# Scaling of token tiles moved from VectorE to POOL in the first stage of a hybrid decoder step

## The chip, the cores and the metric

The kernel runs on one core of one Trainium2 chip. The metric is the time of one execution in device microseconds. Of the kernel before there are three timed runs, and one more execution that the hardware profiler recorded.

## The reference

One step of a one-layer decoder with two groups of heads side by side: stick-breaking attention (8 heads of 128) and gated linear attention (4 heads). 16 meta tokens, 1024 prompt tokens and 32 sample tokens (8 sequences of 4) go through the same layer; the sample tokens also attend to 1024 cached keys each. All numbers are float32. The part that matters here is the start, the norm of the input and the shared input projection:

```python
def rms_norm(x, g):
    xf = x.astype(jnp.float32)
    var = jnp.mean(xf * xf, axis=-1, keepdims=True)
    return (xf * lax.rsqrt(var + EPS) * g.astype(jnp.float32)).astype(x.dtype)
...
        h = rms_norm(x, norm_pre_g[l])
...
    u = h @ w_in
```

Here x has 1072 rows of 2048 numbers, and w_in has 2048 x 7184. The outputs are the new token rows, the new keys and values and the new states.

## The kernel before, in words

A float32 product is made of three faster ones: each operand is split into an upper half (its value rounded to the fp32r format) and a lower half (what the rounding left), and TensorE adds up upper x upper, upper x lower and lower x upper.

**First stage (lines 189 to 277).** The tokens lie in nine tiles, 0 to 8, of 128 rows (tile 0 has the 16 meta tokens ahead of 112 prompt rows; tile 8 has the last 16 prompt rows and the 32 sample rows, folded so that it needs one buffer of 1024 columns instead of two). `load_x(i)` (line 197) issues a tile's transfers. For tile 8 POOL first clears rows that no transfer fills (a memset, line 201), and the transfers of the sample rows on the SP queue (line 210) wait for it. `norm_x(i)` (line 215) makes the tile's norm and scales it:

- ScalarE squares each piece and sums it up (line 225), and VectorE adds up the pieces (line 227). For tile 8 VectorE also adds the two folded halves (lines 231 to 233).
- `rstd_` (line 156) makes one over the root: a multiply-add on VectorE (line 162), a logarithm and an exponential on ScalarE (lines 163, 164), and four tiny VectorE operations that refine it (lines 165 to 168).
- line 236 multiplies the tile by this number, row by row, in place: two instructions of 128 x 1024 (one of 112 x 1024 for tile 8).

Three groups of tiles, c = 0, 1, 2 (tiles 0-2, 3-5, 6-8), follow one another. In each, for 16 blocks of 128 columns, TensorE transposes the block of three tiles into a PSUM buffer `tx` (line 260; five such buffers), ScalarE copies it to SBUF times the weight `gpre`, which is the upper half in `hT` (line 261), and VectorE makes the lower half from the same PSUM buffer (line 262). A `tx` buffer is free for a later block when line 262 has read it. The products with the first 128 columns of w_in (`acc_v`, lines 272 to 274) are mixed in among the transposes. `NORMS` (line 238) says behind which block which tile's `norm_x` is written: tile 3 behind block 1 of group 0, tiles 4 and 5 behind its blocks 4 and 10, tiles 6, 7 and 8 behind blocks 2, 5 and 8 of group 1. Tiles 0 to 2 are scaled ahead of everything.

**What sets the order.** Each engine works through its own queue in order. The code's order is a start only: a scheduler places the instructions of all engines by priorities and by the times it expects, so an edit of one line moves others. Weight loads are marked urgent. The constants' transfers (lines 140 to 144) are on SP behind tile loads and weight loads; among them is nbal (line 141, 128 x 4 numbers), which VectorE negates (line 142) at a place in its queue amid the lower halves.

Behind this stage come the other column blocks of w_in (lines 279 to 295), with the attention work woven in, and then the output projection. The DVE of the profile is VectorE, ACT is ScalarE, PE is TensorE, SP is the queue that issues most transfers.

Of the kernel before, what the change touches and what calls it, by code (L numbers as in the profile page):

```python
# [16 lines left out]
ALU = mybir.AluOpType  # L17
# [65 lines left out]
def hybrid_step(ctx: ExitStack, tc: tile.TileContext, x_prompt, x_sample, cache_k, cache_v, state_gla,  # L83
# [5 lines left out]
    vec, act, pool = nc.vector, nc.scalar, nc.gpsimd  # L89
# [66 lines left out]
    def rstd_(pl, ssq, n, rows, w, nm):  # L156

        v = pl.tile([P, w], F32, tag="rs_v", name=f"v_{nm}")
        r = pl.tile([P, w], F32, tag="rs_r", name=f"r_{nm}")
        t = pl.tile([P, w], F32, tag="rs_t", name=f"t_{nm}")  # L160
        v, r, t = v[:rows], r[:rows], t[:rows]
        vec.tensor_scalar(v, ssq, 1.0 / n, EPS, ALU.mult, ALU.add)
        act.activation(r, v, AF.Ln)
        act.activation(r, r, AF.Exp, scale=-0.5)
        vec.tensor_tensor(t, r, r, ALU.mult)
        vec.tensor_tensor(t, t, v, ALU.mult)
        vec.tensor_scalar(t, t, -0.5, 1.5, ALU.mult, ALU.add)
        vec.tensor_tensor(r, r, t, ALU.mult)
        return r
# [20 lines left out]
    with tc.tile_pool(name="xp", bufs=2) as xp, tc.tile_pool(name="xps", bufs=5, space=PSUM) as xps:  # L190
# [24 lines left out]
        def norm_x(i):  # L215
            xt = xts[i]
            rows = P if i < 8 else 112
            w = H if i < 5 else 512 if i < 8 else 256
            q = len(xt) * H // w
            ssq = xp.tile([P, 4], F32, tag="ssq", name=f"ssq{i}")  # L220
            for e in range(q):
                j0 = 0 if i < 5 else (448 if i < 8 else 768) + 1088 * (e % 2)
                jk = hT[15][:rows, j0:j0 + w]
                xe = xt[e * w // H][:rows, e * w % H:e * w % H + w]
                act.activation(jk, xe, AF.Square, accum_out=ssq[:rows, e:e + 1])
            sq = xp.tile([P, 1], F32, tag="sq", name=f"sq{i}")
            vec.tensor_reduce(sq[:rows], ssq[:rows, :q], mybir.AxisListType.X, ALU.add)
            if i == 8:
                other = xp.tile([P, 1], F32, tag="so", bufs=1, name="so")
                pool.memset(other[:], 0.0)  # L230
                vec.tensor_copy(other[0:48], sq[64:112])
                vec.tensor_copy(other[64:112], sq[0:48])
                vec.tensor_tensor(sq[:rows], sq[:rows], other[:rows], ALU.add)
            r = rstd_(xp, sq[:rows], D, rows, 1, f"x{i}")
            for t in xt:
                vec.tensor_scalar(t[:rows], t[:rows], r, None, ALU.mult)

        NORMS = {(0, 1): 3, (0, 4): 4, (0, 10): 5, (1, 2): 6, (1, 5): 7, (1, 8): 8}
        for i in range(5):
# [6 lines left out]
        for i in range(3):  # L246
            norm_x(i)
        for c, (lo, hi) in enumerate(CHUNKS):
            n = hi - lo
            for k in range(NK):  # L250
                ps = xps.tile([P, 384], F32, tag="tx", name=f"tx{c}_{k}")
                ks = slice(k % 8 * P, (k % 8 + 1) * P)
                for j in range(3):
                    xt = xts[3 * c + j]
                    if len(xt) == 2:
                        src, ii = xt[k // 8][:, ks], ident[:]
                    else:
                        rs = slice(64 * (k // 8), 64 * (k // 8) + 48)
                        src, ii = xt[0][rs, ks], ident[rs, rs]
                    nc.tensor.transpose(ps[:, j * P:min((j + 1) * P, n)], src, ii)  # L260
                act.activation(hh[k][:, lo:hi], ps[:, :n], AF.Copy, scale=gpre[:, k:k + 1])
                vec.scalar_tensor_tensor(hl[k][:, lo:hi], ps[:, :n], gpre[:, k:k + 1], hh[k][:, lo:hi].bitcast(F32),
                                         ALU.mult, ALU.subtract)
                if c == 0 and k == 7:
                    load_x(5)
                if (c, k) in NORMS:
                    norm_x(NORMS[c, k])
            lo, hi = SCHUNKS[c]
            o_ = first[c][:, :hi - lo]
            for k in range(NK):  # L270
                wh, wl = (t[:, k % 2, :] for t in wchunks[k // 2])
                mm(o_, wh, hh[k][:, lo:hi], start=(k == 0), stop=False)
                mm(o_, wh, hl[k][:, lo:hi], start=False, stop=False)
                mm(o_, wl, hh[k][:, lo:hi], start=False, stop=(k == NK - 1))
            if c == 0:
                for i in (6, 7, 8):
                    load_x(i)
# [1264 lines left out]
```

## Time and profile before

| what | us |
|---|---|
| median of three runs | 2131.66 |
| lowest and highest of them | 2129.86, 2132.66 |
| the profiled execution's own time | 2132.25 |
| its span, first to last instruction | 2130.5 |
| TensorE busy in the span | 2066.0 (97%) |
| VectorE busy | 1573.2 (74%) |
| ScalarE busy | 994.4 (47%) |
| POOL busy | 81.9 (4%) |

The span is the time from the first to the last instruction; the execution's own time has 1.75 us around it. Shares of busy time are means over all stages. What the first stage does is read from the timeline of its first 74 us, where each row gives an instruction's start, its length, and in brackets how long its engine had stood idle ahead of it and which instruction or transfer ended that.

### The profile page before, as it was taken

How to read it: one execution, taken by the hardware profiler on the slowest of the kernel's cores; microseconds unless marked ns; L12 is line 12 of the kernel's file. 1: busy time of each engine (PE TensorE's matmuls, PEld its weight loads, DVE VectorE, ACT ScalarE, POOL GpSimd, SP SyncE). 2: the span in 40 equal slices, each digit the busy share in tenths (PEclk: the TensorE clock that was granted, in tenths of full speed). 3: DMA queues.
4: the chain of work that ended last, by engine and by line, in shares of the span. 5: the costliest groups of instructions: out<-in, count | busy, mean ns of one | idle time of the engine just before them, and what ended most of it. 6: DMA issues, size and time to landing. Idle time of an engine off the chain costs nothing.

```text
span 2130.5 us, 43361 instructions
## 1 busy us (share of the span) xinstructions
PE 2066.0 (97%) x12546; PEld 1868.5 (88%) x12546; DVE 1573.2 (74%) x6592; ACT 994.4 (47%) x2536; POOL 81.9 (4%) x298
## 2 busy tenths in 40 slices
PE   5999999999999999999999999999999999999997
PEld 5999999999999989999898998998888887777775
DVE  6368888889888889898897888977544446453575
ACT  7345556565555656424435345353434335342332
POOL 0000000100001010200000000000000000000000
PEclk9999999999999999999999999999999999999999
DMA  6234443444444354554443444336667666452484
GB/s 198 72 100 126 129 129 108 135 130 114 132 131 123 104 143 115 163 132 114 120 121 111 134 116 132 94 86 186 206 220 236 216 190 195 134 154 76 128 286 168
DMA packets 380442, 304.02 MB, mean 143 GB/s; under 512 B 50410, under 2 KB 320682, under 8 KB 380202
## 3 DMA queue, kind: packets, MB, share of 16 engines
q1 hardware_dynamic: 378010, 300.97, 48.6%
q8 instruction: 99, 1.62, 0.3%
q14 instruction: 141, 1.16, 0.2%
q10 hardware_dynamic: 2192, 0.27, 0.1%
HBM read 243.39 MB, written 57.72 MB: 141 GB/s over the span
## 4 chain that ended last, share of the span: by engine, by line
PE 81%; DVE 8%; DMA 7%; issue 2%; ACT 2%; SPq 1%; POOL 0%; DVEq 0%; ACTq 0%; POOLq 0%
PE acc_g L289 4%; PE b L1451 4%; PE acc_g L291 4%; PE acc_g L290 4%; PE b L1452 4%; PE b L1453 4%; PE acc_k L289 3%; PE acc_k L290 3%; PE acc_k L291 3%; PE acc_q L289 3%; PE acc_q L290 3%; PE acc_q L291 3%; PE acc_gv L289 3%; PE acc_gv L290 3%; PE acc_gv L291 3%; PE acc_v L289 3%
## 5 line engine op out<-in xcount | busy, mean ns | idle before, releaser
L384 DVE SCALAR_TENSOR_TENSOR jk<-kp,qb 128x128 f32<-128x128 f32 x2048 | 591.1, 289 | 39.0 <-DMA qb<-qsd 2.0
L289 PE MATMUL acc_g<-hT,wh_g 128*128 128x368 f32 (+2 forms) x768 | 252.9, 329 | 3.2 <-ACT gx L438 3.1
L291 PE MATMUL acc_g<-hT,wl_g 128*128 128x368 f32 (+2 forms) x768 | 247.3, 322 | 0.0
L290 PE MATMUL acc_g<-hT,wh_g 128*128 128x368 f32 (+2 forms) x768 | 247.2, 322 | 0.0
L1451 PE MATMUL b<-ring,f 128*128 128x512 f32 x416 | 166.6, 402 | 6.0 <-ACT gx L438 2.9
L289 PEld LDWEIGHTS acc_g<-hT,wh_g 128*128 128x128 f32 x768 | 144.3, 188 | 28.7 <-ACT wh_g L184 15.9
L1315 DVE TENSOR_TENSOR ring<-wr,ring 128x512 fp32r<-128x512 f32 x104 | 70.7, 690 | 133.0 <-ACT ring L1314 132.4
L384 DVE DVE_READ_ACCUMULATOR jk<-kp,qb 128x1 f32 x2048 | 166.5, 81 | 0.0
L1452 PE MATMUL b<-ring,f 128*128 128x512 f32 x416 | 163.1, 392 | 0.9 <-DVE ring L1315 0.9
L1453 PE MATMUL b<-ring,f 128*128 128x512 f32 x416 | 162.8, 391 | 0.0
L291 PEld LDWEIGHTS acc_g<-hT,wl_g 128*128 128x128 f32 x768 | 144.3, 188 | 1.6 <-issue 1.6
L290 PEld LDWEIGHTS acc_g<-hT,wh_g 128*128 128x128 f32 x768 | 144.4, 188 | 1.0 <-issue 0.3
L1314 ACT CAST ring<-wr 128x512 fp32r<-128x512 f32 x104 | 64.3, 621 | 163.9 <-DMA wr<-in_w_out_dram 79.4
L289 PE MATMUL acc_gv<-hT,wh_gv 128*128 128x384 f32 (+1 forms) x384 | 129.2, 336 | 0.0
L289 PE MATMUL acc_k<-hT,wh_k 128*128 128x378 f32 (+1 forms) x384 | 127.6, 332 | 0.0
L290 PE MATMUL acc_k<-hT,wh_k 128*128 128x378 f32 (+1 forms) x384 | 125.4, 326 | 0.0
L289 PE MATMUL acc_q<-hT,wh_q 128*128 128x368 f32 (+2 forms) x384 | 125.3, 326 | 0.0
L291 PE MATMUL acc_gv<-hT,wl_gv 128*128 128x384 f32 (+1 forms) x384 | 125.3, 326 | 0.0
L291 PE MATMUL acc_k<-hT,wl_k 128*128 128x378 f32 (+1 forms) x384 | 125.2, 326 | 0.0
L290 PE MATMUL acc_gv<-hT,wh_gv 128*128 128x384 f32 (+1 forms) x384 | 124.7, 325 | 0.0
L290 PE MATMUL acc_q<-hT,wh_q 128*128 128x368 f32 (+2 forms) x384 | 123.6, 322 | 0.0
L291 PE MATMUL acc_q<-hT,wl_q 128*128 128x368 f32 (+2 forms) x384 | 123.5, 322 | 0.0
(427 smaller groups left out, 5401.7 us busy)
## 6 DMA issues: line engine op xcount, KB each, us to landing
kp<-in_cache_k_dram SPq DMA_DIRECT2D x512, 64.0 KB
vr<-in_cache_v_dram SPq DMA_DIRECT2D x64, 512.0 KB
tf<-in_w_out_dram SPq DMA_DIRECT2D x64, 256.0 KB
qb<-qsd SPq DMA_DIRECT2D x64, 256.0 KB
td<-tf SPq DMA_DIRECT2D x64, 256.0 KB
wr_g<-in_w_in_dram SPq DMA_DIRECT2D x128, 128.0 KB
wr<-td SPq DMA_DIRECT2D x64, 256.0 KB
wr<-in_w_out_dram SPq DMA_DIRECT2D x48, 256.0 KB
```

Of the source, the lines that this page charges most:

```text
L289: mm(acc[c][:, :n], wh[:, k2, :], hh[k][:, lo:hi], start=(k == 0), stop=False)
L290: mm(acc[c][:, :n], wh[:, k2, :], hl[k][:, lo:hi], start=False, stop=False)
L291: W.mark = mm(acc[c][:, :n], wl[:, k2, :], hh[k][:, lo:hi], start=False, stop=(k == NK - 1)).ins
L384: ins = vec.scalar_tensor_tensor(jk[:], kp[:], 1.0, qbs[h, b][:, t, :], ALU.mult, ALU.mult, accum_out=zt[:, t, NPG - 1 - i:NPG - i])
L1314: act.copy(wh, r)
L1315: vec.tensor_tensor(wl, r, wh.bitcast(F32), ALU.subtract)
L1451: mm(bk[:], ah, wh, start=first and k == 0, stop=False, skip_group_check=True)
L1452: mm(bk[:], ah, wl, start=False, stop=False, skip_group_check=True)
L1453: mm(bk[:], al, wh, start=False, stop=last and k == 7, skip_group_check=True)
```

## The change

One line of `norm_x`: tiles 0 to 2 are still scaled by VectorE, tiles 3 to 8 by POOL.

```diff
@@ -233,7 +233,7 @@
             r = rstd_(xp, sq[:rows], D, rows, 1, f"x{i}")
             for t in xt:
-                vec.tensor_scalar(t[:rows], t[:rows], r, None, ALU.mult)
+                (vec if i < 3 else pool).tensor_scalar(t[:rows], t[:rows], r, None, ALU.mult)
```

With it the scheduler moves other instructions of this stage; behind the stage every engine's order is as it was, and SP's order is the same throughout.

POOL, from the end of the identity matrix on. The names `x_0_` and `x_1_` are the two halves of a tile's row: 233 and 234 are tile 3, 237 and 238 tile 4, 374 and 375 tile 5, and 501 is tile 8.

```order
 masks.py:199 AFFINE_SELECT ident<-ident 128x128
+L236 TENSOR_SCALAR x_0_233<-x_0_233,r_x_310 128x1024
+L236 TENSOR_SCALAR x_1_234<-x_1_234,r_x_310 128x1024
+L236 TENSOR_SCALAR x_0_237<-x_0_237,r_x_345 128x1024
+L236 TENSOR_SCALAR x_1_238<-x_1_238,r_x_345 128x1024
 L201 MEMSET x_0_501 32x1024
+L236 TENSOR_SCALAR x_0_374<-x_0_374,r_x_404 128x1024
+L236 TENSOR_SCALAR x_1_375<-x_1_375,r_x_404 128x1024
```

The memset for tile 8, which was POOL's first instruction behind the identity, now stands behind four scalings. Behind the rows shown come the two scalings of tile 6, the two of tile 7 and the one of tile 8.

VectorE, at the change from group 0 to group 1. `hT_162` is the last block of group 0, `hT_147`, `hT_148`, `hT_149` are the first three of group 1; `sq_530` and `v_x_532` belong to the norm of tile 6.

```order
 L262 SCALAR_TENSOR_TENSOR hT_162<-tx_15_439,gpre,hT_162 128x384
-L167 TENSOR_SCALAR t_x_405<-t_x_405 128x1
-L168 TENSOR_TENSOR r_x_404<-r_x_404,t_x_405 128x1
-L236 TENSOR_SCALAR x_0_374<-x_0_374,r_x_404 128x1024
-L236 TENSOR_SCALAR x_1_375<-x_1_375,r_x_404 128x1024
+L262 SCALAR_TENSOR_TENSOR hT_147<-tx_0_507,gpre,hT_147 128x384
+L142 TENSOR_SCALAR nbal<-nbal 128x4
+L262 SCALAR_TENSOR_TENSOR hT_148<-tx_1_513,gpre,hT_148 128x384
+L262 SCALAR_TENSOR_TENSOR hT_149<-tx_2_519,gpre,hT_149 128x384
 L227 TENSOR_REDUCE sq_530<-ssq_525 128x1
 L162 TENSOR_SCALAR v_x_532<-sq_530 128x1
-L142 TENSOR_SCALAR nbal<-nbal 128x4
```

Tile 5's scaling is gone from here (its norm's last steps stand earlier now). The operation on nbal moved behind the first lower half of group 1, and tile 6's sum and variance moved behind nbal and two more lower halves.

ScalarE, at the same place. The `L225` rows are the squares of tile 6, `r_x_533` its norm.

```order
 L225 ACTIVATE hT_162,ssq_525<-x_0_493 128x512 x2
-L225 ACTIVATE hT_162,ssq_525<-x_1_494 128x512 x2
+L225 ACTIVATE hT_162,ssq_525<-x_1_494 128x512
 L261 ACTIVATE hT_147<-tx_0_507,gpre 128x384
 L261 ACTIVATE hT_148<-tx_1_513,gpre 128x384
 L261 ACTIVATE hT_149<-tx_2_519,gpre 128x384
+L225 ACTIVATE hT_162,ssq_525<-x_1_494 128x512
+L261 ACTIVATE hT_150<-tx_3_544,gpre 128x384
+L261 ACTIVATE hT_151<-tx_4_550,gpre 128x384
 L163 ACTIVATE r_x_533<-v_x_532 128x1
-L261 ACTIVATE hT_150<-tx_3_544,gpre 128x384
+L261 ACTIVATE hT_152<-tx_5_556,gpre 128x384
```

The last of tile 6's four squares moved behind the first three copies of group 1, and the logarithm of its norm behind two more. On TensorE the transposes of tile 5's first two blocks moved ahead, among group 0's last products, and two of tiles 3 and 4 went behind them; on VectorE the operation of line 233 (tile 8's two halves) moved ahead of group 1's tenth lower half, and TensorE transposes tile 8's first block as its third transpose of group 2, where it stood behind seven others.

## The prediction

> **What bounds the kernel now.** I read the page's head, then TensorE's waits in the first 74 us (where every instruction of the change lies), the chain of waits, and the busy time stretch by stretch.
>
> ```profile
> span 2130.5 us, 43361 instructions
> PE 2066.0 (97%) x12546; PEld 1868.5 (88%) x12546; DVE 1573.2 (74%) x6592; ACT 994.4 (47%) x2536; POOL 81.9 (4%) x298
> ```
>
> TensorE is busy 97% of the span. So the change is worth what it takes from TensorE's idle time between 26 us (first edited scaling) and 58 us. These are TensorE's rows around its waits there, in the timeline (start, length, idle time before, releaser):
>
> ```profile
> 36.31 0.44 PE L272 MATMUL acc_v<-hT,wf 128*128 128x378 f32 x1 [1.75 <-ACT hT L261]
> 41.38 0.27 PE L260 MATMUL tx<-ident,x 128*128 128x128 f32 x1
> 44.84 0.55 PE L260 MATMUL tx<-ident,x 128*128 128x128 f32 x3 [1.30 <-DVE hT L262]
> 53.57 0.55 PE L260 MATMUL tx<-ident,x 128*128 128x128 f32 x3 [0.84 <-DVE hT L262]
> 57.99 2.13 PE L260 MATMUL tx<-ident,x 128*128 128x128 f32 x14
> ```
>
> Two waits, 1.30 and 0.84 us, end with VectorE: 2.14 us is what VectorE can give at most. The 1.75 us ends with ScalarE, and behind that stands a transfer of weights, which the change doesn't touch; the second row is a stretch of time (busy PE, PEld, DVE, ACT, POOL, then granted clock, DMA share, GB/s):
>
> ```profile
> 34.94 0.84 ACT L184 CAST wh_k<-wr_k 128x256 fp32r<-128x256 f32 x2 [1.37 <-DMA wr_k<-in_w_in_dram]
> 37.60:41.20 3.60, 3.60 (x16) 3.42 (x15) 3.42 (x10) 3.54 (x12) 0.00 (x0) 0.53 1.04 202
> ```
>
> After that pause TensorE had 0.53 of its clock for 3.6 us, which costs it 3.6 x 0.47 = 1.7 us. Both stay: in the new order one small ScalarE instruction (L163 for tile 5, 0.2 us) goes ahead of the copy that ends the pause, no more. Should the new order bring a second pause of that kind, 1.7 us is its price. The other stretches:
>
> ```profile
> 44.00:46.00 2.00, 1.16 (x9) 1.13 (x10) 1.90 (x6) 1.69 (x6) 0.00 (x0) 1.00 0.00 0
> 46.00:52.00 6.00, 6.00 (x44) 5.71 (x43) 5.83 (x18) 5.97 (x23) 0.00 (x0) 1.00 0.00 0
> 52.00:54.00 2.00, 1.16 (x9) 0.85 (x8) 1.92 (x7) 2.00 (x5) 0.00 (x0) 1.00 0.00 0
> 58.00:74.00 16.00, 16.00 (x98) 12.92 (x97) 8.91 (x19) 8.68 (x19) 1.00 (x8) 1.00 0.00 1
> ```
>
> From 44 to 54 us ScalarE is as full (9.66 of 10) as VectorE (9.65); from 58 us on TensorE has no gap. The chain there, in order of time:
>
> ```profile
> 37.69 6.39 DMA nbal<-in_b_alpha_dram
> 44.10 0.17 DVE nbal L142
> 44.27 1.57 DVE hT L262 x3
> 47.71 1.42 DVE x L236 x2
> 51.51 1.42 DVE x L236 x2
> 52.99 0.54 DVE hT L262
> ```
>
> VectorE stands still until the tiny transfer of nbal lands at 44.1, since L142 waits for it at the head of its queue; then two scaled pairs (2.84 us) lie on the chain.
>
> **The change: VectorE.** One line's instructions (min/median/max ns):
>
> ```profile
> L236 DVE TENSOR_SCALAR x<-x,r_x x17: 746/752/755, 12.2 to 57.8; 128x1024 f32<-128x1024 f32 x16, 112x1024 f32<-112x1024 f32 x1
> ```
>
> Eleven of the 17 leave VectorE: 11 x 0.75 = 8.3 us, 2.84 of it on the chain. No transfer, copy or matmul goes away.
>
> **POOL's price** for such a scaling is not in the trace. Its nearest rows (mean ns behind the bar), and the memset ahead of tile 8:
>
> ```profile
> L1096 POOL MEMSET vn<- 128x1024 f32 x1 | 0.9, 947 | 0.0
> L517 POOL TENSOR_SCALAR_AFFINE_SELECT X<-X 127x126 f32<-127x126 f32 x48 | 14.3, 298 | 66.9 <-DVE X L514 63.7
> L517 POOL TENSOR_SCALAR_AFFINE_SELECT X<-X 25x24 f32<-25x24 f32 x8 | 1.6, 204 | 183.4 <-DVE X L514 183.4
> L704 POOL TENSOR_SCALAR_AFFINE_SELECT lv<-lv 128x64 f32<-128x64 f32 x14 | 6.0, 452 | 0.1
> 33.48 1.31 POOL L201 MEMSET x<- 32x1024 f32 x1 [32.10 <-PE tx L260]
> ```
>
> Lower end: a write of the same width, which reads nothing, 0.95 us. Through the two L517 rows a pass that reads and writes costs 0.18 + 0.92 ns a column: 1.1 us for 1024, the value I take. Upper end: L704 takes 1.9 times that line (0.45 for 0.24), so 2.1 us. Call the price s.
>
> **Where a slow POOL shows first.** SP issues nbal behind tile 8's transfers, which wait for that memset, and POOL's memset now stands behind tile 4's two scalings.
>
> ```profile
> 26.51 1.42 DVE L236 TENSOR_SCALAR x<-x,r_x 128x1024 f32<-128x1024 f32 x2
> 32.28 0.16 DVE L168 TENSOR_TENSOR r_x<-r_x,t_x 128x1 f32<-128x1 f32 x1
> 39.61 0.16 DVE L168 TENSOR_TENSOR r_x<-r_x,t_x 128x1 f32<-128x1 f32 x1
> 34.81 0.89 SPq L210 DMA_DIRECT2D x<-in_x_sample_dram  x2
> 35.83 0.90 SPq L180 DMA_DIRECT2D wr_k<-in_w_in_dram  x2
> ```
>
> The first row is tile 3's pair, the L168 rows end tile 4's and tile 5's norms. Tile 4's is ready at 32.4, and some 0.4 earlier without tile 3's pair ahead: 32.0 (an estimate). SP issued nbal at 37.69 (chain, above). The memset ends at 32.0 + 2s + 0.95 instead of 34.8; SP needs 1.9 us from there until it is free for nbal (34.81 to 36.73), and stood idle for 0.96 more. With s = 1.1 it ends at 35.15: 0.36 late, nbal on time, cost nothing. With s = 2.1 nbal is 1.4 us late, and VectorE, ScalarE and TensorE with it. With s = 0.95 nothing is gained by it, since SP stood idle before nbal already. Queued behind nbal on SP are two tiny transfers and then cache pages, which wait for the end of this stage.
>
> **What goes, and what is late next.** VectorE now makes the first lower half (hT_147) ahead of its wait for nbal, so TensorE's next three transposes and two matmuls (44.84 to 45.57, 0.73 us) go into its 1.30 us wait. But the other wait hangs on ScalarE too:
>
> ```profile
> 42.47 1.52 ACT L261 ACTIVATE hT<-tx,gpre 128x384 fp32r<-128x384 f32 x3 [1.33 <-PE tx L260]
> 45.90 0.62 ACT L225 ACTIVATE hT<-x 128x512 fp32r<-128x512 f32 x1
> 48.36 1.03 ACT L261 ACTIVATE hT<-tx,gpre 128x384 fp32r<-128x384 f32 x2
> 51.68 3.05 ACT L261 ACTIVATE hT<-tx,gpre 128x384 fp32r<-128x384 f32 x6
> ```
>
> TensorE now transposes tile 5 where the lone transpose of 41.38 stood, so ScalarE's copies start at about 41.5, not 42.47. (Tile 5 must be scaled by then: its norm was there at 39.77, plus 1.1 is 40.9.) Three copies (1.52), the one square of tile 6 that is moved behind them (0.62) and two copies (1.0) bring it to 44.6. There L163 for tile 6 now waits for VectorE: nbal at 44.27, two halves (1.05), reduce and scale (0.3) give 45.6. Then L163 and L164, a copy (0.9 together) and tile 7's squares, which start at about 46.5 instead of 45.90. So everything behind is 0.6 us later on ScalarE, and its copy of 51.68 starts at 52.3. That copy (0.5) and its lower half (0.54) end at 53.4, where the chain has 53.53. The 0.84 us wait hardly shrinks; the 0.73 us is given back as another wait. Sum of the likeliest case: -0.1 to -0.3, I take **-0.2 us**.
>
> Tile 8 is the last that could be late: its scaling ended VectorE's part at 58.5 (row below); POOL has it at about 56.2 + 1.1, ahead of TensorE's need at 58. POOL's five scalings from tile 6's norm on (row at 47.53) end at 47.5 + 5s, so they are late only from s = 2.1.
>
> ```profile
> 47.53 0.15 DVE L168 TENSOR_TENSOR r_x<-r_x,t_x 128x1 f32<-128x1 f32 x1
> 57.77 0.76 DVE L236 TENSOR_SCALAR x<-x,r_x 112x1024 f32<-112x1024 f32 x1
> 313.08 0.69 POOL L517 TENSOR_SCALAR_AFFINE_SELECT X<-X 33x32 f32<-33x32 f32 x1 [13.35 <-DVE X L514]
> 313.08 0.41 DVE L185 TENSOR_TENSOR wl_v<-wr_v,wh_v 128x256 fp32r<-128x256 f32 x1
> ```
>
> **Contention.** The last two rows: a POOL select of 33x32 took 0.69 while VectorE ran a two-input operation of 0.41; the 25x24 ones above take 0.20. The two can hold each other up. VectorE's L233, two inputs, now stands ahead of the half of 52.99 while tile 7 is scaled: 0 to 1.1 us late, and I count 0. The Trainium skill (SBUF — State Buffer, Who interferes with whom) speaks against the change: a VectorE operation with two SBUF inputs and a POOL operation that reads SBUF exclude each other for a whole instruction. The trace agrees (0.69 for 0.20); by that rule the sum would be up to +0.9.
>
> So the bounds are -0.73 (none given back) and +1.4 + 1.1 = +2.5. The profiled execution took 2132.25 us, 1.75 over its span, 0.59 above the median of 2131.66; -0.2 makes it 2132.05, and the median **2131.5**.
>
> **Rivals.**
> 1. VectorE alone was the limit and both waits go: -2.1, 2129.5. For it: both end with L262. Against it: ScalarE's 9.66 of 10. Chance 0.10.
> 2. POOL is so slow that it becomes the bound: with s above 2.1 nbal is 2s - 2.8 late and tile 8 another 5s - 10.5. At s = 2.5 that is 2.2 + 2.0 = 4.2, which is 0.2%; at 3.0 it is 3.2 + 4.5 = 7.7: 2139.4. For it: a POOL pass with a scalar by partition is nowhere in the trace. Against it: 1.1 by the L517 rows. Chance of s above 2.5: 0.07; between 1.5 and 2.5 (2132 to 2136): 0.10.
> 3. POOL's first such instruction starts late by some t, as if code had to be fetched: tile 4 is then done at 26.5 + t + 4s, the memset 0.95 and nbal's issue another 1.9 later, so with s = 1.1 nbal is late by t - 3.9. Rows of a first use (POOL's first select, ScalarE's load of its table):
>
> ```profile
> 1.08 0.29 POOL masks.py:199 TENSOR_SCALAR_AFFINE_SELECT ident<-ident 128x128 f32<-128x128 f32 x1
> 1.73 1.28 ACT L97 ACT_TABLE_LOAD   x1 [1.73 <-PEq L1523]
> ```
>
> The first select took what later ones take, so t = 0; with ScalarE's load, t = 1.3, nothing is late either: 2131.5. From t = 8.2 on it passes 4.3 us: 2135.9. Chance that t is above 3.9: 0.03. The Trainium skill (GPSIMD Engine Reference, Instruction dispatch) gives about 6 us for the first call of a freshly loaded library; by that it would be 2.1 us, 2133.8, and no row here shows such a load.
>
> That nothing moves is excluded: POOL's order has all eleven scalings, and VectorE's has none of them left.
>
> **How the numbers follow.** My case has 0.68, the rivals 0.30, anything else 0.02. About 0.2% (4.3 us) is what a measurement of this kernel can tell from no change. Faster by that would need more than the 2.14 us: 0.03. Slower: rival 2 beyond 2.5 and a little else, 0.08. Same: 0.89. The range takes in rival 1 and, with the runs' own spread (2129.86 to 2132.66), the slower POOL: 2128.8 to 2135.
>
> **What would show it.** Right: eleven L236 rows on POOL near 1.1 us; nbal issued near 37.7; TensorE's 0.84 us wait replaced by one ended by ScalarE, and 58 to 74 us as full. Wrong: POOL rows above 2 us, nbal late, or TensorE at its 57.99 row over 1 us earlier.

## The result, and the profile after

| | before | after |
|---|---|---|
| median of 6 runs, us | 2132.02 | 2147.00 (2143.69 to 2152.38) |
| profiled execution, us | 2132.25 | 2146.43 |
| its span, us | 2130.5 | 2144.7 |
| mean granted TensorE clock | 0.994 | 0.989 |

After takes 1.0076 of before, with an interval of 1.0065 to 1.0087: 15 us slower, where 2131.5 was forecast and the range ended at 2135. The head of the page of after:

```profile
span 2144.7 us, 43378 instructions
PE 2077.1 (97%) x12546; PEld 1875.4 (87%) x12546; DVE 1568.1 (73%) x6581; ACT 994.7 (46%) x2536; POOL 112.3 (5%) x309
```

TensorE has the same 12546 matmuls and is busy 11.1 us longer (2066.0 before): most of the loss is not idle time but the same work done slower. The change's own line in after (min/median/max ns, first and last start):

```profile
L236 POOL TENSOR_SCALAR x<-x,r_x x11: 2842/2846/2964, 26.5 to 59.0; 128x1024 f32<-128x1024 f32 x10, 112x1024 f32<-112x1024 f32 x1
L236 DVE TENSOR_SCALAR x<-x,r_x x6: 745/750/753, 12.3 to 18.6; 128x1024 f32<-128x1024 f32 x6
```

A scaling costs 2.85 us on POOL and 0.75 us on VectorE. The forecast took 1.1 us, with 2.1 as its upper end. POOL's timeline in after (start, length, idle time before, releaser):

```profile
26.49 5.67 POOL L236 TENSOR_SCALAR x<-x,r_x 128x1024 f32<-128x1024 f32 x2 [25.12 <-DVE r_x L168]
32.37 5.79 POOL L236 TENSOR_SCALAR x<-x,r_x 128x1024 f32<-128x1024 f32 x2 [0.21 <-ACT hT L225]
38.21 0.94 POOL L201 MEMSET x<- 32x1024 f32 x1
39.25 5.67 POOL L236 TENSOR_SCALAR x<-x,r_x 128x1024 f32<-128x1024 f32 x2
47.72 14.13 POOL L236 TENSOR_SCALAR x<-x,r_x 128x1024 f32<-128x1024 f32 x5 [2.80 <-ACT hT L225]
```

The last row is tiles 6, 7 and 8 without a gap: five scalings end at 61.85. TensorE's timeline around them:

```profile
45.02 0.55 PE L260 MATMUL tx<-ident,x 128*128 128x128 f32 x3 [0.24 <-DVE hT L262]
53.31 0.55 PE L260 MATMUL tx<-ident,x 128*128 128x128 f32 x3 [0.35 <-DVE v_x L162]
57.61 0.27 PE L260 MATMUL tx<-ident,x 128*128 128x128 f32 x1
61.90 3.80 PE L260 MATMUL tx<-ident,x 48*128 48x48 f32 x13 [4.03 <-POOL x L236]
87.91 0.33 PE L289 MATMUL acc_k<-hT,wh_k 128*128 128x378 f32 x1
```

The two waits that ended with VectorE are down from 1.30 and 0.84 us to 0.24 and 0.35. TensorE reaches group 2 (the third group of token tiles, 6 to 8) at 57.61, the place that stands at 57.99 in before; after one more transpose it has nothing to do for 4.03 us until tile 8 is scaled. Behind that, the stretches of time (columns: busy PE, PEld, DVE, ACT, POOL, then granted clock, DMA share, GB/s):

```profile
58.00:74.00 16.00, 12.10 (x40) 7.70 (x41) 5.34 (x10) 5.31 (x11) 4.55 (x5) 0.63 0.00 1
61.90:86.00 24.10, 24.10 (x82) 17.45 (x83) 8.54 (x16) 9.16 (x18) 0.70 (x3) 0.50 0.00 1
86.00:88.00 2.00, 2.00 (x15) 2.00 (x15) 0.33 (x2) 0.03 (x1) 0.31 (x5) 0.99 0.00 0
```

For 24.1 us TensorE is busy without a gap, at half its clock; before, 58 to 74 us stood at 1.00. The ledger up to acc_k's first matmul (87.91; before 73.76):

- TensorE reaches group 2 at 57.61 instead of 57.99: -0.4.
- It goes on at 61.90, after one transpose and the wait of 4.03 us: +4.3.
- Group 2 takes 61.90 to 87.91 = 26.0 instead of 57.99 to 73.76 = 15.8: +10.2.

The sum is +14.1, and the span of the profiled execution is 14.2 longer: in the end nothing is given back later.

### The profile page after: what moved, and what is told of

Read it like the earlier page. It is cut to its first block, busy times and chain, and to the rows that moved or that the text cites. A ratio compares the mean times of both kernels' runs of the same rounds, so it can differ in the third digit from the quotient of the medians.

```text
span 2144.7 us, 43378 instructions
## 1 busy us (share of the span) xinstructions
PE 2077.1 (97%) x12546; PEld 1875.4 (87%) x12546; DVE 1568.1 (73%) x6581; ACT 994.7 (46%) x2536; POOL 112.3 (5%) x309
## 4 chain that ended last, share of the span: by engine, by line
PE 85%; DVE 6%; DMA 5%; ACT 2%; issue 1%; POOL 1%; SPq 0%; DVEq 0%; ACTq 0%; POOLq 0%
PE acc_g L289 5%; PE acc_g L291 5%; PE acc_g L290 5%; PE b L1451 4%; PE b L1452 4%; PE b L1453 4%; PE acc_k L289 3%; PE acc_k L290 3%; PE acc_k L291 3%; PE acc_q L289 3%; PE acc_q L290 3%; PE acc_q L291 3%; PE acc_v L289 3%; PE acc_gv L289 3%; PE acc_gv L290 3%; PE acc_gv L291 3%
## 5 line engine op out<-in xcount | busy, mean ns | idle before, releaser
L289 PEld LDWEIGHTS acc_g<-hT,wh_g 128*128 128x128 f32 x768 | 144.9, 189 | 28.8 <-ACT wh_g L184 14.2
```

The costliest lines, as they stand in the source:

```text
L289: mm(acc[c][:, :n], wh[:, k2, :], hh[k][:, lo:hi], start=(k == 0), stop=False)
```

## The experiments

The theory after the result: POOL is slow enough that tile 8 is late, that pauses TensorE, and the pause brings half clock, which lasts because of what runs behind it. The rivals: tile 8 is late only because POOL and VectorE hold each other up (B); the scalings of tiles 3 to 5 build the loss (C); the lower clock comes from something other than the pause (D). Times beside each kernel are those of the kernel before on the same chip. In the four kernels with inserted matmuls or POOL multiplications the lines behind them carry numbers 3 higher. The code shown is cut to the lines that differ.

**The price of POOL's scaling.** The kernel before, with five operations on a scratch tile at the program's start (VectorE has nothing to do there until 8.8 us; the four lines that make and fill the tiles are left out):

```diff
...
+        pool.tensor_scalar(scr[:], scr[:], one[:], None, ALU.mult)
+        pool.tensor_scalar(scr[:], scr[:], 1.5, None, ALU.mult)
+        pool.tensor_scalar(scr[:, :256], scr[:, :256], one[:], None, ALU.mult)
+        pool.tensor_copy(scr[:, :512], scr[:, 512:])
+        pool.tensor_tensor(scr[:, :512], scr[:, :512], scr[:, 512:], ALU.mult)
```

> The kernel before with POOL operations on a scratch tile early in its idle time (their results aren't used): a scaling of 128x1024 by a number per partition, by a constant, one of 128x256, a copy of 128x512 and a product of two 128x512 tensors. If the price lies in the columns (2.78 ns each, whatever the scalar): 2.85 us for both of 1024, 0.7 to 0.8 for 256. If it lies in the scalar by partition: the constant one costs about 1.1 us, as the rows of the select suggested. The time itself: as before, POOL waits for nothing there.

POOL's timeline in it:

```profile
2.38 2.85 POOL L242 TENSOR_SCALAR scr<-scr,one 128x1024 f32<-128x1024 f32 x1
5.31 2.77 POOL L243 TENSOR_SCALAR scr<-scr 128x1024 f32<-128x1024 f32 x1
8.18 0.93 POOL L244 TENSOR_SCALAR scr<-scr,one 128x256 f32<-128x256 f32 x1
9.16 0.61 POOL L245 COPY scr<-scr 128x512 f32<-128x512 f32 x1
9.86 1.27 POOL L246 TENSOR_TENSOR scr<-scr 128x512 f32<-128x512 f32 x1
```

The price is the same 2.85 us with VectorE idle, and almost the same with a constant for the scalar by partition (2.77). It lies mostly in the columns: (2.85 - 0.93) / 768 = 2.5 ns each, and the rest, 0.93 - 256 x 2.5 ns = 0.29 us, is why 256 columns take more than the 0.7 to 0.8 expected. A copy is cheaper: 0.61 us for 512 columns, where this line gives 1.6. So contention does not make POOL's price, and the select rows of the forecast were rows of a cheaper kind of work. The kernel's one execution took 2130.94 us (before 2128.93).

**All but tile 8's scaling on POOL.**

```diff
-                (vec if i < 3 else pool).tensor_scalar(t[:rows], t[:rows], r, None, ALU.mult)
+                (vec if i < 3 or i == 8 else pool).tensor_scalar(t[:rows], t[:rows], r, None, ALU.mult)
```

> Tiles 3 to 7 are scaled on POOL, tile 8 on VectorE again: ten of the eleven scalings stay where the change put them. Theory A (the loss is the wait of TensorE for tile 8, which stands last in POOL's queue at 2.85 us each, and the half clock behind it): the wait of 4.03 us and the low clock are gone, 2131.6, within 0.2% of before, TensorE at the end of group 1 still 0.4 us earlier than before. Rival B (POOL's scalings hold up VectorE's two-input operations and the loss builds up over all tiles): most of it stays, 10/11 of 14 us, about 2145.

Measured: 2129.19 us (before 2128.93), ratio 1.0009 (0.9998 to 1.0019). POOL's last scalings, TensorE's start of group 2 and one stretch behind it (columns as in the stretches of after):

```profile
47.04 11.32 POOL L236 TENSOR_SCALAR x<-x,r_x 128x1024 f32<-128x1024 f32 x4 [2.73 <-ACT hT L225]
```

```profile
56.99 2.69 PE L260 MATMUL tx<-ident,x 128*128 128x128 f32 x14
```

```profile
62.00:66.00 4.00, 4.00 (x23) 2.93 (x22) 2.62 (x6) 2.64 (x6) 0.70 (x3) 1.00 0.00 0
```

TensorE starts group 2 without a wait and 1.0 us earlier than before, and the clock stays at 1.00 behind it. With ten of the eleven scalings still on POOL, the loss is gone as far as these runs can tell: by the interval the ten others cost at most 4 us of the 15. So rival B falls.

**Tiles 6 to 8 on POOL, and tiles 3 to 5 on POOL.** Two kernels, each with half of the change:

```diff
+                (pool if i > 5 else vec).tensor_scalar(t[:rows], t[:rows], r, None, ALU.mult)
```

> Only tiles 6, 7 and 8 are scaled on POOL. Theory A: POOL's five scalings start when tile 6's norm is ready at 47.5 and end at 47.5 + 14.1 = 61.6, tile 8 is as late as with the whole change: about 2146, with the wait of 4 us and the low clock. Rival C (the loss comes from tiles 3 to 5, through the memset and the nbal transfer behind them): within 1 us of before. Rival B: half of the loss, 2138 to 2140.

```diff
+                (pool if i in (3, 4, 5) else vec).tensor_scalar(t[:rows], t[:rows], r, None, ALU.mult)
```

> Only tiles 3, 4 and 5 are scaled on POOL, tiles 6, 7 and 8 on VectorE. Theory A: no loss, since POOL's queue is empty long before tile 8, and no gain above 1 us, since ScalarE sets group 1's pace: within 2 us of before. Rival C (loss through the memset and nbal behind tile 4's scalings): 2 to 4 us slower.

Tiles 6 to 8 alone: 2142.04 us (before 2128.93), ratio 1.0068 (1.0052 to 1.0084), nearly the whole loss. Its row at the start of group 2 in TensorE's timeline:

```profile
61.84 3.73 PE L260 MATMUL tx<-ident,x 48*128 48x48 f32 x13 [3.51 <-POOL x L236]
```

The same wait, and half clock from 62.2 to 82.6 us. Rival C falls as the cause of the loss. Tiles 3 to 5 alone: 2131.67 us (before 2128.37), ratio 1.0020 (1.0010 to 1.0030), 3.3 us where at most 2 was expected. TensorE's and POOL's rows there:

```profile
41.54 0.33 PE L260 MATMUL tx<-ident,x 128*128 128x128 f32 x1 [2.69 <-POOL x L236]
53.53 0.55 PE L260 MATMUL tx<-ident,x 128*128 128x128 f32 x3 [0.77 <-DVE hT L262]
```

```profile
38.64 5.66 POOL L236 TENSOR_SCALAR x<-x,r_x 128x1024 f32<-128x1024 f32 x2
```

TensorE waits 2.69 us for tile 5, whose scalings are queued behind tile 4's and the memset, but the wait of 1.30 us at 44.84 is absent there and acc_k starts at 73.7, as before (73.8). The profiled execution (2129.55) is one of the shortest of its nine, so where the others lose 3 us is not seen and stays open.

**Only tile 8's scaling on POOL.**

```diff
+                (pool if i == 8 else vec).tensor_scalar(t[:rows], t[:rows], r, None, ALU.mult)
```

> Only tile 8 is scaled on POOL, 2.85 us instead of 0.76 on VectorE. Its norm is ready at about 57.6 as before, POOL is done at 60.5; TensorE has the transposes of tiles 6 and 7 ahead until about 59, so it pauses for some 1.5 us. If a pause of this size leaves a stretch of half clock of some 4 us, as the pause of 1.75 us at 36 us did: 1.5 + 1.7 = 3 us slower than before. If any pause ahead of group 2 leaves the whole of group 2 at half clock: 1.5 + 10 = 11 to 12 us slower.

Measured: 2138.85 us (before 2128.37), ratio 1.0035 (1.0019 to 1.0051). POOL, TensorE and the granted clock (busy PE ahead of it) in the profiled execution:

```profile
58.40 2.84 POOL L236 TENSOR_SCALAR x<-x,r_x 112x1024 f32<-112x1024 f32 x1 [23.45 <-DVE r_x L168]
```

```profile
61.30 1.00 PE L260 MATMUL tx<-ident,x 48*128 48x48 f32 x7 [1.84 <-POOL x L236]
```

```profile
62.00:63.00 1.00, 0.91 (x4) 0.86 0.00 0
63.00:64.00 1.00, 1.00 (x4) 0.50 0.00 0
...
78.00:79.00 1.00, 1.00 (x5) 0.50 0.00 0
79.00:80.00 1.00, 1.00 (x6) 0.61 0.00 0
80.00:81.00 1.00, 1.00 (x9) 1.00 0.00 0
```

One instruction of 2.84 us, a pause of 1.84 us, then 17 us at half clock, and acc_k starts at 83.34 (before 73.76): 9.6 us later, 7.7 more than the pause. That is near the longer of the two expected prices. Over all its runs the interval says 4.0 to 10.9 us, between the two prices, because not all runs are alike: two of the ten took 2129.24 and 2131.20 at a mean clock of 0.995 and 0.996, the other eight 2133.7 to 2140.5 at 0.988 to 0.991: a pause of this length apparently does not always bring the low clock, though no profile shows such a run of this kernel.

**The change, with TensorE kept busy in the pause.** 25 matmuls ahead of group 2, whose result is overwritten; and the same 25 in the kernel before, for their own price:

```diff
+            if c == 2:
+                for _ in range(25):
+                    mm(first[2][:, :378], wf[:, 0, :], hh[15][:, 384:762], start=True, stop=True)
```

> The whole change, with 25 extra matmuls (which leave nothing behind, their bank is started anew) put ahead of group 2, so that TensorE works while tile 8 is scaled. Theory A with the clock as the second half of the loss: the 4.3 us go by with TensorE busy, the clock stays at 1.0 and group 2 runs as before: loss 4 us, 2136. Rival D (group 2 is slow for another reason than a pause, the matmuls only stand in the place of the wait): 24 us at half clock stay, 2146 or more.

> The kernel before with the same 25 extra matmuls ahead of group 2, where TensorE has no pause: what 4.3 us of TensorE's time in this place cost at the end. If every later stage follows TensorE: 4.3 us slower than before. If later waits take some of it in, as the 1.8 us of the changed kernel with the extra matmuls hints: 1 to 3 us.

The change with them takes 2130.71 us (before 2128.93), ratio 1.0008 (0.9999 to 1.0017). TensorE's rows and one stretch (columns as in the stretches of after):

```profile
58.03 4.31 PE L252 MATMUL acc_v<-hT,wf 128*128 128x378 f32 x24
62.18 2.81 PE L263 MATMUL tx<-ident,x 128*128 128x128 f32 x15
```

```profile
66.00:74.00 8.00, 8.00 (x46) 5.75 (x44) 5.25 (x11) 5.28 (x11) 0.70 (x3) 1.00 0.00 0
```

```profile
48.01 14.14 POOL L236 TENSOR_SCALAR x<-x,r_x 128x1024 f32<-128x1024 f32 x5 [3.16 <-ACT hT L225]
```

POOL ends tile 8 at 62.15, as late as in the change, but TensorE comes out of useless work instead of a pause, and the clock stays at 1.00. 4 us of added work takes away 10 us of half clock: the pause is the cause, and rival D falls. The same work in the kernel before takes 2135.34 (before 2128.37), ratio 1.0035 (1.0021 to 1.0050), more than the 4.3 us that it lasts. Both kernels start acc_k at the same time (78.6 and 78.7, 4.9 us later than in before), but end 4.6 us apart in their medians; so the change with the matmuls ends nearer to its kernel before than the 4 us expected for a reason that lies behind this stage. The two kept traces show where their executions (2129.41 and 2135.34 us) part: at waits of TensorE that end at 1484, 1757 and 2073 us. In the kernel before with the matmuls these waits take 1.88, 2.89 and 2.08 us, and behind each stands 3.4 us of half clock; in the other they take 1.78, 1.75 and 0.95 us, and the clock stays at 1.00. The distance grows there by 1.6, 2.6 and 1.2 us. Why the waits differ stays open, and whether the other runs part in the same places is not known.

**What ends the half clock: 25 matmuls in its middle.** The change, with 25 matmuls in a row behind group 2's first transposes:

```diff
+                if c == 2 and k == 0:
+                    for _ in range(25):
+                        mm(first[2][:, :304], wf[:, 0, :], hh[0][:, 768:1072], start=True, stop=True)
```

> The whole change, with 25 extra matmuls (they leave nothing behind) behind the first ten transposes of group 2, after the wait for tile 8. Theory: the clock comes back only when TensorE runs matmuls back to back, which group 2's mix of short transposes and matmuls isn't; then the burst brings it back after some 4 us, its 25 matmuls take about 5 us, the rest of group 2 runs at full clock: 10 to 11 us slower than before instead of 14 to 15. Rival: the clock comes back a fixed 24 us after the pause, whatever runs: the burst adds its 6 us at half clock, 20 us slower than before.

Measured: 2137.10 us (before 2128.37), ratio 1.0047 (1.0029 to 1.0065). TensorE and the clock:

```profile
61.61 2.51 PE L260 MATMUL tx<-ident,x 48*128 48x48 f32 x8 [3.97 <-POOL x L236]
63.78 5.79 PE L266 MATMUL acc_v<-hT,wf 128*128 128x304 f32 x25
69.41 2.69 PE L260 MATMUL tx<-ident,x 128*128 128x128 f32 x14
```

```profile
67.00:68.00 1.00, 1.00 (x6) 0.50 0.00 0
68.00:69.00 1.00, 1.00 (x8) 0.83 0.00 0
69.00:70.00 1.00, 1.00 (x9) 1.00 0.00 0
```

After 4.6 us of matmuls the clock is back (63.78 to about 68.3), and it stays at 1.00 through the same mix of transposes and matmuls that ran at 0.50 in the change. So the stretch has no fixed length, and the mix does not lower the clock; it only fails to raise it. With 25 matmuls too many the change costs 8.7 us over its kernel before (6 to 14 by the interval); without them it cost 15.0 (14 to 19).

**A pause of the same length where only matmuls follow.** The kernel before, in which POOL multiplies the last lower half of group 2 by 1.0 seven times:

```diff
+            if c == 2:
+                for _ in range(7):
+                    pool.tensor_scalar(hl[15][:, lo:hi], hl[15][:, lo:hi].bitcast(F32), 1.0, None, ALU.mult)
```

> The kernel before, with a pause of TensorE of the same length put 12 us later: POOL multiplies the lower half of the last transposed tile, group 2's part (304 columns), by 1.0 seven times, so that TensorE's last hT_162 matmul of group 2 (before: 73.47 us) waits. The half is there at 70.25; seven such passes at 1.05 us (0.93 for 256 columns, 2.5 ns for each more) end at 77.8: a pause of about 4.2 us, as long as that of the changed kernel, but with only back-to-back matmuls behind it (acc_k). Theory (the clock falls after the pause and comes back after 2.2 to 4.8 us of back-to-back matmuls, as it did in the four kernels in which it fell in group 2; what made it 24 us is the mix of short transposes behind the pause): 4.2 plus half of 2.2 to 4.8, so 5.3 to 6.6 us over the kernel before. Rival (any pause of that length costs some 20 us of half clock, whatever comes behind it): 4.2 plus 10, so 14.

Measured: 2135.56 us (before 2129.63), ratio 1.0028 (1.0016 to 1.0039), so 3.4 to 8.3 us. TensorE and the clock:

```profile
78.30 0.63 PE L276 MATMUL acc_v<-hT,wh_v 128*128 128x316 f32 x1 [3.73 <-POOL hT L270]
...
83.46 0.36 PE L294 MATMUL acc_k<-hT,wl_k 128*128 128x316 f32 x1
83.66 0.34 PE L292 MATMUL acc_k<-hT,wh_k 128*128 128x378 f32 x1
```

```profile
82.00:83.00 1.00, 1.00 (x6) 0.50 0.23 66
83.00:84.00 1.00, 1.00 (x6) 0.72 0.23 66
84.00:85.00 1.00, 1.00 (x7) 1.00 0.00 0
```

A pause of 3.73 us, then 5.3 us at half clock instead of 24: 3.73 + 2.6 = 6.3 us, between the 5.3 and 6.6 of the theory and far from the rival's 14. (The half clock lasted a little longer than the 4.8 us expected at most.) The same pause costs less than half as much some 16 us later in the program.

## Why the prediction was wrong

**The step that failed first: "POOL's price", "1.1 us for 1024, the value I take".** It measured 2.85 us, and 2.1 was no upper end. The line through the two L517 rows was a line through selects of 126 and 24 columns; a multiplication costs 2.5 ns a column and not 0.92. In the same prediction stood L704, a POOL row that took 1.9 times that line: a sign that POOL's price a column depends on the operation, read as an end of the range and not as a reason to distrust the line. The Trainium skill (GPSIMD Engine Reference, Elementwise — side-by-side cycle accounting) gives 4497 ns for a two-input addition of 2048 columns on this engine; half of it, 2.25 us, would be an estimate nearer to the 2.85 than any row of the trace of before, though for another operation. The trace agrees roughly on the two-input kind: 1.27 us for 512 columns in the kernel with the scratch tile, 1.12 as an estimate by that figure.

**Rival 2 was the mechanism, and half of it.** It had a chance of 0.07 beyond 2.5 us. Its part on tile 8 is right to a tenth: "five scalings from tile 6's norm on (row at 47.53) end at 47.5 + 5s", which with 2.85 is 61.8, and 61.85 was measured. Its part on nbal did not occur, though SP did issue it late; these are SP's queue and VectorE in after:

```profile
41.44 0.46 SPq L141 DMA_DIRECT2D nbal<-in_b_alpha_dram  x1
```

```profile
43.93 1.01 DVE L142 TENSOR_SCALAR nbal<-nbal 128x4 f32<-128x4 f32 x1 [0.17 <-DMA nbal<-in_b_alpha_dram]
```

Issued 3.75 us later than before (37.69), it was there at 43.93 (44.10 before): 2.5 us on its way instead of 6.39. Before, it went out into a stretch in which the DMA share was 1.04, in after into one of 0.63 (41.4 to 43.9); that this is why was not tested. The forecast added a late issue to a late landing as if the time on the way were fixed.

**The second failed step: "Should the new order bring a second pause of that kind, 1.7 us is its price."** With the measured 2.85, rival 2's formula gives 2.9 + 3.75 = 6.7 us, and without nbal 3.75; 14.2 came. What is missing is the 10.2 us that half clock costs. The forecast had its price from the one pause in sight, at 36 us, whose half clock lasted 3.4 us, and left even that price out of rival 2, which lets TensorE wait for tile 8 and then run on at full speed. The price belonged to what ran behind that pause, not to the pause: the kernel with the late pause pays 2.6 us for its half clock and after 10.2, behind pauses of 3.73 and 4.03 us.

**What was right.** The gain at the start of group 2 was taken as -0.2 and was -0.4, well short of the 2.14 that VectorE's waits added up to. The way was not quite the one described: the wait of 0.84 us was to be replaced by one that ends with ScalarE, and it shrank to 0.35 and still ends with VectorE. Nothing starts late at POOL's first scaling (its first pair took 5.67, as the third did), so rival 3 does not occur. Contention is there, as the row of L142 just shown says (1.01 us for 128x4, 0.17 before), and VectorE, rid of 8.3 us of scalings, is busy only 5.1 us less (1573.2 to 1568.1). It may be behind the wait of 0.83 us that TensorE now has for VectorE at 37.28 (0.21 at 36.96 before); from 42 us on no wait of TensorE for VectorE is over 0.35. The kernel with ten scalings on POOL, whose VectorE work is stretched by as much (1569.0 us busy, where 7.5 us less than before would be 1565.7), loses nothing that its runs can tell.

## What to carry to other kernels

Price an operation that moves to another engine by that operation on that engine, alone and at two sizes; a line through rows of another operation was wrong by a factor of 2.6 here, and five such errors in a queue add up before the one consumer that has no slack. Look at the last of the moved instructions first: with it back on VectorE the ten others cost nothing that the runs can tell; with it alone on POOL 4 to 11 us were lost, and the four queued ahead of it made it later still. Price a pause of TensorE by the pause and by how soon a run of back-to-back matmuls stands behind it, not by its length alone.

## What the runs showed of the hardware

- **The half clock lasts as long as the work behind the pause lets it, and in steps of 3.41 us.** In finer windows of the traces its stretches last one step (before, 37.8 to 41.2), two (6.8 us: the 25 matmuls in the middle, the late pause), five (17.1: tile 8 alone), six (20.5: tiles 6 to 8) and seven (23.9: after). Back-to-back matmuls ended it after 2.0 us (tiles 6 to 8: 80.7 to 82.6), 2.3 (tile 8 alone: 77.5 to 79.8), 4.6 (the 25 matmuls in the middle), 5.3 (the late pause) and 5.2 (after: 80.8 to 86.0); some of this spread may be the rest of a step. Group 2's mix, in which three 128x316 matmuls share 2.8 us with six transposes, had not ended it after 19 us. The Trainium skill (TensorE: Matmul & The Clock Gate, What's actually happening) puts the return of the clock at about 3.4 us of sustained activity, counted in windows that run on by themselves, and in Part 4: PE-mode transpose says that transposes do not count as busy in the same way; the steps agree with the windows, by the first alone the stretch would be over within two of them and is not, and the second agrees with the mix at 0.50. It is not the whole story: in the early pauses of these kernels (45 us in the one with tile 8 alone) a mix with wider matmuls (378 columns) and quicker transposes (three in 0.50 us, against 0.83 in group 2, both at half clock) was back at full clock after some 4 us. Where the border between the two mixes lies was not tried.
- **A pause of 1.84 us was enough** in the profiled execution with tile 8 alone, and one of 1.75 us at 36 us in before. The two waits of 1.30 and 0.84 us in before were not, and neither was one of 2.29 us there that ended at 1752.8: the clock stayed at 1.00 until 1778.6. So length alone does not decide. If the steps run on through the whole execution, a border between two of them cuts that pause into 0.8 and 1.5 us, while the pause of 1.84 us lies in one step (59.3 to 62.7); that would also fit the two short runs with tile 8 alone. This is worked out from the places where the clock changed, and was not tested.
- **POOL's elementwise prices** for fp32 on 128 partitions: 2.85 us for a product with a scalar at 1024 columns, 0.93 at 256, 0.61 for a copy of 512, 1.27 for a two-input product of 512. VectorE's product took 0.75 at 1024.
